# The order of the 24 products of a projected piece: low parts of the weights last

## The chip, the cores and the metric

The kernel runs on one core of a Trainium2 chip. The metric is device time in microseconds (us), from one launch. The engines are named as the profile names them: PE (TensorE, matrix products), PEld (its weight loads), DVE (VectorE), ACT (ScalarE), POOL (GpSimd) and SP (SyncE, which only issues DMAs here).

## What is computed

One layer of a hybrid sequence model on 1024 frames plus 16 learned ones (L = 1040), model width 1024. A normalised input goes through one combined projection, three groups of heads mix it in time, each in its own way, and one output projection brings it back.

```python
hn = rms_norm(h, norm_pre[l])
proj = jnp.einsum("bld,dp->blp", hn, w_in[l])
p_a, p_b, p_c = jnp.split(proj, _splits([P_A, P_B, P_C]), axis=-1)
mixed = jnp.concatenate([
    gated_deltanet_group(p_a, ...),   # 6 heads of 128
    rwkv7_group(p_b, ...),            # 8 heads of 64
    mamba2_group(p_c, ...),           # 12 heads of 64
], axis=-1)
out = jnp.einsum("blm,md->bld", mixed, w_out[l])
h = h + rms_norm(out, norm_post[l])
```

## The kernel before

**The projection.** The projected channels are cut into 61 tiles of 128. A tile is projected by `proj` in two or three pieces of 320 to 512 frames, each into a PSUM tile `pj` of its own (tag "proj", four of them). To keep float32 precision with fast products, the input is held as a rounded part `hh` and a low part `hl`, the weights as a rounded part `w[:, 0]` and a low part `w[:, 1]`, and a piece is the sum of three kinds of products over eight slices `kt` of 128 input channels: rounded weights with `hh`, rounded weights with `hl`, low parts with `hh`. That makes 24 products for a piece, accumulated in one PSUM tile.

**The weights.** `weights` (L143 to L155) fetches a tile in two halves (slices 0 to 3 and 4 to 7), `w_0` and `w_1`. For each half SP loads `raw`, ACT writes the negative of the rounded part to `w[:, 1]` (L151), then the rounded part to `w[:, 0]` (L152), and a DMA issued by POOL adds the float32 weights onto `w[:, 1]` (L153), which leaves the low part. There are four such buffers, so two tiles' weights; a half's buffer is free when the last product that reads it has run. The next tile's weights are asked for after the first piece of a tile (`self.prefetch`).

**What follows a piece.** `evac` empties the PSUM tile on ACT and DVE: a short convolution (`conv`, L179 to L187) or a token shift (`shifted`, L613 and L614).

**The order of the work.** Heads are handled by generators (`unit_a`, `unit_b`, `unit_c` for the three groups, `unit_o` for the output projection). `schedule` calls one step of a scan, or one product of a tile, at a time, by a clock of its own that adds up the size of the products; so small products of the scans (64 by 64 and 32 by 32, in plain float32: `bsi`, `bu`, `bm`, `am` and so on) stand between the large ones of the projection. The framework's scheduler then lays the instructions of each engine in an order for good, by priorities and its own estimate of when operands are there; on the chip every engine runs its instructions in that order, with waits where an operand or a buffer is not there yet. Products called through the class `Meter` all carry line L97.

Of the kernel before, what the change touches and what calls it, by code (L numbers as in the profile page):

```python
# [22 lines left out]
KT = 8  # L23
# [78 lines left out]
class Trunk:  # L102
# [54 lines left out]
    def proj(self, i, pieces, evac, halo=0):  # L157

        w = self.fetched.pop(i, None) or self.weights(i)
        for n, (a, b) in enumerate(pieces):  # L160
            a0 = max(a - halo, 0)
            p = self.pp.tile([128, 512], F32, tag="proj", name=f"pj{i}_{n}")
            for kt in range(KT):
                for m, (x, h) in enumerate(((0, self.hh), (0, self.hl), (1, self.hh))):
                    self.engines[2].matmul(p[:, : b - a0], w[kt // 4][:, x, kt % 4, :], h[:, kt, a0:b],
                                           start=(kt == 0 and m == 0), stop=(kt == KT - 1 and m == 2))
                    yield
            with self.tc.high_priority(EVA):
                evac(p, a, b, a - a0)
            if n == 0:  # L170
                self.prefetch(i)
# [1227 lines left out]
```

## Time and profile before

| | |
|---|---|
| median of 3 runs | 1450.17 us (1448.45 to 1453.15) |
| the profiled execution | 1442.35 us, its span 1440.4 us |
| PE busy | 1389.7 us, 96% of the span |
| weight loads (PEld) | 1188.8 us, beside PE |
| DVE, ACT, POOL busy | 935.4, 719.9, 172.4 us |
| mean granted TensorE clock | 0.985 |

The span counts from the first to the last instruction of the program; the 1.95 us that the time has on top lie around it. The projection lasts from about 23 to 1223 us, and the output projection fills most of what is left. Matmul records overlap (a product's record is about twice as long as the distance to the next one), so PE's speed is read from start to start, and PE's busy share hides waits shorter than a record.

### The profile page before, as it was taken

The numbers are of one execution on the slowest core, as the hardware profiler recorded it, in microseconds if no ns is written. First come the engines' busy times: TensorE is split into PE (matmuls) and PEld (weight loads), VectorE is DVE, ScalarE is ACT, GpSimd is POOL, SyncE is SP. The second block draws the span as 40 slices with busy tenths as digits, with TensorE's granted clock in tenths as the row PEclk, the third lists the DMA queues.
The fourth block names the chain that finished last, engine by engine and source line by source line (L and its number), as shares of the span: only waits on it lengthen the run. The fifth ranks groups of instructions, "written<-read, shape, count | busy, mean of one in ns | idle before, by whom it ended". The sixth has DMA issues, their size and how long they took to land.

```text
span 1440.4 us, 28351 instructions
## 1 busy us (share of the span) xinstructions
PE 1389.7 (96%) x10801; PEld 1188.8 (83%) x10801; DVE 935.4 (65%) x2610; ACT 719.9 (50%) x2020; POOL 172.4 (12%) x223
## 2 busy tenths in 40 slices
PE   4999999999999999999999999999999999899997
PEld 4999888778788789979778898889998987677786
DVE  6548586467667348879625788655589876632663
ACT  6365445446364464545636655444666355632520
POOL 2111010000010011111001110001231110201000
PEclk9999999999999999999979999999999999999999
DMA  7354243213234143234422242234553322743861
GB/s 233 78 131 87 56 102 71 57 40 88 44 66 112 30 133 89 57 82 89 100 60 60 54 108 62 59 88 89 133 124 77 71 38 56 233 133 101 254 198 44
DMA packets 120458, 136.43 MB, mean 95 GB/s; under 512 B 39867, under 2 KB 72379, under 8 KB 120323
## 3 DMA queue, kind: packets, MB, share of 16 engines
q1 hardware_dynamic: 102755, 102.64, 24.1%
q0 software_dynamic: 17568, 31.99, 13.4%
q8 instruction: 85, 1.39, 0.4%
q14 instruction: 50, 0.41, 0.1%
HBM read 116.99 MB, written 17.60 MB: 93 GB/s over the span
## 4 chain that ended last, share of the span: by engine, by line
PE 78%; issue 6%; ACT 6%; DMA 4%; DVE 4%; POOL 0%; SPq 0%; DVEq 0%; ACTq 0%; POOLq 0%
PE pj L97 45%; PE po L97 5%; PE bsi L97 4%; PE bu L97 3%; PE bgr L97 3%; PE am L97 2%; PE aops L97 1%; PE cdg L97 1%; ACT bbt L97 1%; DMA or<-in_w_out_dram 1%; PE ads L97 1%; PE av L97 1%; DMA omrw<-d_mix 1%; PE aks L97 1%; PE agk L97 1%
## 5 line engine op out<-in xcount | busy, mean ns | idle before, releaser
L97 PE MATMUL pj<-hh,w 128*128 128x350 f32 (+7 forms) x2736 | 757.6, 348 | 0.2 <-ACT hh L264 0.2
L97 PEld LDWEIGHTS pj<-hh,w 128*128 128x128 f32 x2736 | 483.4, 190 | 25.7 <-issue 4.4
L97 PE MATMUL pj<-hl,w 128*128 128x350 f32 (+7 forms) x1368 | 474.8, 347 | 0.0
L97 PEld LDWEIGHTS pj<-hl,w 128*128 128x128 f32 x1368 | 260.2, 190 | 11.8 <-issue 1.2
L153 POOL DMA_DIRECT2D w<-in_wt_dram x122 | 106.5, 873 | 878.6 <-ACT w L151 600.5
L151 ACT ACTIVATE w<-wr 128x512 fp32r<-128x512 f32 x122 | 76.8, 630 | 72.7 <-PE pj L97 70.7
L97 PE MATMUL po<-ow,omw 128*128 128x512 f32 x408 | 97.7, 400 | 4.0 <-ACT omw L1088 3.2
L97 PEld LDWEIGHTS po<-ow,omw 128*128 128x128 f32 x408 | 77.5, 191 | 24.2 <-ACT omw L1088 3.6
L97 PE MATMUL po<-ow,ome 128*128 128x512 f32 x360 | 90.5, 402 | 2.1 <-ACT ome L1088 1.6
L97 PEld LDWEIGHTS po<-ow,ome 128*128 128x128 f32 x360 | 66.6, 189 | 17.7 <-ACT ome L1088 2.2
L152 ACT CAST w<-wr 128x512 fp32r<-128x512 f32 x122 | 74.4, 609 | 0.1
L97 DVE TENSOR_SCALAR buv<-bu,b_ib 128x64 f32<-128x64 f32 x68 | 19.2, 282 | 71.6 <-PE bu L97 71.5
L97 PE MATMUL bsi<-buv,bgm 64*64 64x64 f32 x784 | 63.0, 230 | 0.7 <-DVE b_s L97 0.2
L97 DVE TENSOR_TENSOR s_tmp<-alb 33x30 f32<-33x30 f32 (+9 forms) x180 | 57.0, 317 | 3.2 <-DMA alb<-d_l 1.9
L97 DVE TENSOR_TENSOR alb<-alb,s_tmp 33x30 f32<-33x30 f32 (+9 forms) x180 | 57.0, 317 | 3.0 <-POOL alb L97 1.6
L97 PEld LDWEIGHTS bsi<-buv,bgm 64*64 64x64 f32 x784 | 43.5, 136 | 16.5 <-issue 4.6
L184 DVE SCALAR_TENSOR_TENSOR cbc<-pj,pack,cbc 128x346 f32<-128x346 f32 (+4 forms) x72 | 41.1, 571 | 20.5 <-ACT cbc L181 19.7
L852 ACT COPY by<-bsi 64x64 f32<-64x64 f32 x128 | 26.5, 207 | 48.9 <-PE bsi L97 47.6
L1089 DVE TENSOR_TENSOR ome<-omre,ome 128x512 fp32r<-128x512 f32 (+2 forms) x40 | 22.5, 600 | 36.2 <-ACT ome L1088 36.1
L97 PE MATMUL bgr<-bar,bbk 64*64 64x128 f32 x544 | 45.4, 277 | 0.0
L97 PE MATMUL bu<-buv,bbt 64*64 64x64 f32 x512 | 42.4, 234 | 0.0
L184 DVE SCALAR_TENSOR_TENSOR cx<-pj,pack,cx 128x346 f32<-128x346 f32 (+2 forms) x54 | 31.1, 576 | 16.9 <-ACT cx L181 15.9
(324 smaller groups left out, 2390.3 us busy)
## 6 DMA issues: line engine op xcount, KB each, us to landing
wr<-in_wt_dram SPq DMA_DIRECT2D x122, 256.0 KB, 3.4
w<-in_wt_dram POOLq DMA_DIRECT2D x122, 256.0 KB, 4.8
or<-in_w_out_dram SPq DMA_DIRECT2D x32, 256.0 KB, 3.8
omrw<-d_mix SPq DMA_DIRECT2D x32, 256.0 KB, 3.9
clt<-d_cs SPq DMA_DIRECT2D x24, 256.0 KB, 4.9
omre<-d_mix SPq DMA_DIRECT2D x24, 256.0 KB, 2.8
btw<-d_tw SPq DMA_DIRECT2D x8, 544.0 KB, 5.9
x<-in_x_dram SPq DMA_DIRECT2D x8, 512.0 KB, 7.7
```

The costliest lines, as they stand in the source:

```text
L97: return op(out, *args, **kw)
L151: nc.scalar.activation(w[:, 1], raw, AF.Copy, scale=-1.0)
L152: nc.scalar.copy(w[:, 0], raw)
L153: nc.gpsimd.dma_start(w[:, 1], src, accum_op=ADD)
L184: nc.vector.scalar_tensor_tensor(acc[:, a + z: b], p[:, o + z - s: o + b - a - s], cw[:, 3 - s: 4 - s], acc[:, a + z: b], MUL, ADD)
L852: nc.scalar.copy(yt[hs[(c - 1) % 2], (c - 1) // 2, hs[h]], pq[hs[h], 64:128])
L1089: nc.vector.tensor_tensor(t[:, 1], raw, t[:, 0].bitcast(F32), SUB)
```

## The change

The 24 products of a piece get another order. Before, each slice `kt` had its three kinds in turn. Now the 16 products with the rounded weights come first, over all eight slices, and then the eight with the low parts.

```diff
-            for kt in range(KT):
-                for m, (x, h) in enumerate(((0, self.hh), (0, self.hl), (1, self.hh))):
-                    self.engines[2].matmul(p[:, : b - a0], w[kt // 4][:, x, kt % 4, :], h[:, kt, a0:b],
-                                           start=(kt == 0 and m == 0), stop=(kt == KT - 1 and m == 2))
-                    yield
+
+            steps = [(kt, 0, h) for kt in range(KT) for h in (self.hh, self.hl)] + [(kt, 1, self.hh) for kt in range(KT)]
+            for j, (kt, x, h) in enumerate(steps):
+                self.engines[2].matmul(p[:, : b - a0], w[kt // 4][:, x, kt % 4, :], h[:, kt, a0:b],
+                                       start=(j == 0), stop=(j == len(steps) - 1))
+                yield
```

No instruction is added or removed on any engine. Line numbers behind this place are higher by one in the changed kernel.

**First place: PE, the second half of a piece that nothing interrupts** (`pj_1_636` is the piece, `w_0_581` and `w_1_587` its tile's two halves). Before:

```order
L97 MATMUL pj_1_636<-hl,w_0_581 128x350
L97 MATMUL pj_1_636<-hh,w_0_581 128x350
L97 MATMUL pj_1_636<-hh,w_1_587 128x350
L97 MATMUL pj_1_636<-hl,w_1_587 128x350
L97 MATMUL pj_1_636<-hh,w_1_587 128x350 x2
L97 MATMUL pj_1_636<-hl,w_1_587 128x350
L97 MATMUL pj_1_636<-hh,w_1_587 128x350 x2
```

With the change:

```order
L97 MATMUL pj_1_636<-hl,w_0_581 128x350
L97 MATMUL pj_1_636<-hh,w_1_587 128x350
L97 MATMUL pj_1_636<-hl,w_1_587 128x350
L97 MATMUL pj_1_636<-hh,w_1_587 128x350
L97 MATMUL pj_1_636<-hl,w_1_587 128x350
L97 MATMUL pj_1_636<-hh,w_1_587 128x350
L97 MATMUL pj_1_636<-hl,w_1_587 128x350
L97 MATMUL pj_1_636<-hh,w_1_587 128x350
L97 MATMUL pj_1_636<-hl,w_1_587 128x350
L97 MATMUL pj_1_636<-hh,w_0_581 128x350 x4
L97 MATMUL pj_1_636<-hh,w_1_587 128x350 x4
```

The last product that reads the first half `w_0` was the 12th of the 24 and is now the 20th; the last that reads `w_1` is still the 24th.

**Second place: ACT, from the 54th row of its order on, during the first DeltaNet tile** (`pj_0_593`, `pj_1_636` and `pj_2_667` are its pieces, `w_0_766` is the first half of a later tile, which takes over the buffer of `w_0_581`). Before:

```order
L151 ACTIVATE w_0_766<-wr_0_767 128x512
L353 ACTIVATE sc_ecs<-sc_cs 128x162
L152 CAST w_0_766<-wr_0_767 128x512
L179 ACTIVATE ak_580<-pj_0_593,pack 128x348
L179 ACTIVATE ak_580<-pj_1_636,pack 128x346
```

With the change:

```order
L354 ACTIVATE sc_ecs<-sc_cs 128x162
L180 ACTIVATE ak_580<-pj_0_593,pack 128x348
L180 ACTIVATE ak_580<-pj_1_636,pack 128x346
L352 ACTIVATE sc_kd<-sc 128x54
L353 ACTIVATE sc_kdt<-sc 128x108
L355 ACTIVATE sc_etot<-pcl 128x162
L151 ACTIVATE w_0_766<-wr_0_767 128x512
L180 ACTIVATE ak_580<-pj_2_667,pack 128x346
L152 CAST w_0_766<-wr_0_767 128x512
```

The write to `w_0_766` stood ahead of the emptying of the first two pieces and now stands behind it.

**Third place: ACT and PE in the middle of the program, at an RWKV tile** (`bv` is the tile's result, `pj_1_7922` its second piece, `bvT` are transposes of `bv` on PE, `buv` is where ACT copies them, `cyT` are transposes of another head). ACT before:

```order
L97 COPY buv_0_8133<-bvT_0_8135 64x64 x2
L613 ACTIVATE bv_7362<-pj_1_7922,mu_321 128x384
L97 COPY buv_0_8133<-bvT_1_8151 64x4x64 x3
L97 ACTIVATE cz_6619<-cyT_00_7691,pack 128x512
L97 ACTIVATE cz_6620<-cyT_01_7720,pack 128x512
```

ACT with the change:

```order
L614 ACTIVATE bv_7362<-pj_1_7922,mu_321 128x384
L97 COPY buv_0_8133<-bvT_0_8135 64x64 x2
L97 COPY buv_0_8133<-bvT_1_8151 64x4x64 x4
L97 ACTIVATE cz_6619<-cyT_00_7691,pack 128x512
L97 ACTIVATE cz_6620<-cyT_01_7720,pack 128x512
```

The emptying of the second piece stood behind the copies to `buv` and now stands ahead of them. PE before, in the third piece:

```order
L97 MATMUL cyT_00_7691<-pack,cx_0_5817 128x128
L97 MATMUL cyT_01_7720<-pack,cx_0_5817 128x128
L97 MATMUL pj_2_8048<-hh,w_0_7706 128x322
L97 MATMUL pj_2_8048<-hl,w_0_7706 128x322
L97 MATMUL pj_2_8048<-hh,w_0_7706 128x322 x2
L97 MATMUL bvT_1_8151<-pack,bv_7362 128x128
```

PE with the change:

```order
L97 MATMUL pj_2_8048<-hh,w_1_7712 128x322
L97 MATMUL pj_2_8048<-hl,w_1_7712 128x322
L97 MATMUL bvT_1_8151<-pack,bv_7362 128x128 x2
L97 MATMUL bvT_9_8172<-pack,bv_7362 128x128
L97 MATMUL pj_2_8048<-hh,w_1_7712 128x322
L97 MATMUL pj_2_8048<-hl,w_1_7712 128x322
```

Ten products of the third piece stand ahead of `bvT_1` in both; the two `cyT` have moved behind it, and `bvT_9` has come forward, ahead of the piece's last 14 products.

## Rows read from the trace of the kernel before

**Rows 1.** The page: busy engines, and the chain that ended last.

```profile
PE 1389.7 (96%) x10801; PEld 1188.8 (83%) x10801; DVE 935.4 (65%) x2610; ACT 719.9 (50%) x2020; POOL 172.4 (12%) x223
...
PE 78%; issue 6%; ACT 6%; DMA 4%; DVE 4%; POOL 0%; SPq 0%; DVEq 0%; ACTq 0%; POOLq 0%
```

**Rows 2.** Engines by stretch, 60 to 1225 us: the sum's row.

```profile
sum 1165.00, PE 1150.80 PEld 995.11 DVE 792.80 ACT 610.00 POOL 144.18; mean PE 191.80 PEld 165.85 DVE 132.13 ACT 101.67 POOL 24.03
```

**Rows 3.** PE's waits: who it waited for, us in total, times, longest.

```profile
PE bvT L97 <- DVE bv L614: 2.6, 1, 2.6
...
PE bbT L97 <- ACT bbt L97: 1.5, 5, 0.4
...
PE bu L97 <- ACT b_x L97: 1.0, 2, 0.7
...
PE pj L97 <- ACT hh L264: 0.2, 1, 0.2
```

**Rows 4.** Timeline of PE at 601 us: start, length, instruction, count.

```profile
600.86 0.32 PE L97 MATMUL pj<-hl,w 128*128 128x350 f32 x1
...
601.34 0.32 PE L97 MATMUL pj<-hl,w 128*128 128x350 f32 x1
601.50 0.38 PE L97 MATMUL akT<-pack,ak 128*128 128x128 f32 x2
601.64 0.56 PE L97 MATMUL pj<-hh,w 128*128 128x350 f32 x2
602.04 0.32 PE L97 MATMUL pj<-hl,w 128*128 128x350 f32 x1
```

**Rows 5.** Timeline of PE: second to fifth product of the first piece.

```profile
25.25 0.63 PE L97 MATMUL pj<-hl,w 128*128 128x336 f32 x1
25.67 0.48 PE L97 MATMUL pj<-hh,w 128*128 128x336 f32 x1
...
26.66 0.63 PE L97 MATMUL pj<-hh,w 128*128 128x336 f32 x1
27.09 0.47 PE L97 MATMUL pj<-hl,w 128*128 128x336 f32 x1
```

**Rows 6.** ACT's waits for PE at the weights, and ACT's timeline at 65 us.

```profile
ACT w L151 <- PE pj L97: 70.7, 36, 9.6
...
65.48 0.63 ACT L151 ACTIVATE w<-wr 128x512 fp32r<-128x512 f32 x1 [9.55 <-PE pj L97]
66.02 0.32 ACT L353 ACTIVATE sc_ecs<-sc_cs 128x162 f32<-128x162 f32 x1
```

**Rows 7.** Timelines of SP, ACT, DVE and PE at 685 to 694 us.

```profile
684.73 0.28 SPq L758 DMA_DIRECT2D d_t<-blb  x1
691.85 1.33 SPq L760 DMA_DIRECT2D bgm<-d_t  x3
...
691.90 0.42 ACT L97 COPY buv<-bvT 64x64 f32<-64x64 f32 x2 [5.73 <-issue]
692.35 0.58 ACT L613 ACTIVATE bv<-pj,mu 128x384 f32<-128x384 f32 x1
...
692.96 0.62 DVE L614 SCALAR_TENSOR_TENSOR bv<-pj,pack,bv 128x384 f32<-128x384 f32 x1 [2.87 <-ACT bv L613]
...
688.85 0.31 PE L97 MATMUL pj<-hl,w 128*128 128x322 f32 x1
...
690.61 0.46 PE L97 MATMUL pj<-hh,w 128*128 128x322 f32 x2
693.63 0.47 PE L97 MATMUL bvT<-pack,bv 128*128 128x128 f32 x1 [2.56 <-DVE bv L614]
```

**Rows 8.** Engines by stretch around two falls of the clock (PEclk: share granted).

```profile
693.00:696.40 3.40, 2.77 (x12) 2.68 (x13) 1.95 (x7) 1.58 (x4) 0.00 (x0) 0.50 0.45 69
...
720.30:723.70 3.40, 3.40 (x81) 2.81 (x79) 0.26 (x1) 1.47 (x5) 0.00 (x0) 1.00 0.39 159
723.70:740.80 17.10, 17.10 (x103) 12.30 (x104) 1.93 (x7) 4.89 (x15) 0.86 (x1) 0.50 0.17 32
```

## Prediction

> **What bounds the kernel now.** I read the page first. PE is busy for 1389.7 us of 1440.4, and the chain of work that ended last is 78% PE; ACT stands at half the span and POOL at an eighth [rows 1]. Records of products overlap, so I looked next at how much time PE has nothing in flight: in the whole projection stage, 60 to 1225 us, it is 1165.0 − 1150.8 = 14.2 us, or 1.2% of the stage [rows 2]. The list of PE's waits tells what ended the longer ones. No row of it names a DMA or the weights: the only one at `pj` is 0.2 us, for `hh` [rows 3]. So PE runs an order that was fixed when the program was built, almost without a gap, and its time is the sum of its products, of what it costs to pass between kinds of products, and of the granted clock. A change that adds and removes nothing can move the time in three ways: by a wait it takes away or adds, by more or fewer passages between kinds, and by what the clock makes of the new mixture.
>
> **The products themselves.** In the timeline at 601 us three products of 350 columns, rounded with `hh`, low with `hh` and rounded with `hl` among them, take 601.34 − 600.86 = 0.48 us from start to start, 0.16 us each whatever the kind [rows 4]. Each has its own weight load: 10801 loads for 10801 products [rows 1]. The order of the kinds inside an undisturbed piece is therefore worth nothing, either way; 24 products stay 24 times 0.16 us.
>
> **The low parts are needed later.** They come last of a half's operands, by way of two ACT instructions and POOL's DMA. Before, the third product of a piece reads them, now the 17th, 14 products or 14 × 0.16 = 2.2 us later. That is worth something only where PE waited for them. The place where it is likeliest is the first piece, whose weights have just been fetched: its second product starts at 25.25 and its third, the first that reads low parts, at 25.67, 0.42 us on. But two products further, where nothing new is read, the same distance is 27.09 − 26.66 = 0.43 us [rows 5]. So nothing was waited for even there, and in the remaining tiles, prefetched a tile ahead, the list of waits shows none. I cost this at 0. What covers it before is the prefetch; if that cover were thin, the gain could be at most the 0.2 us of rows 3 and what hides inside a record.
>
> **The first half's buffer comes free later.** Its last reader moves from the 12th to the 20th product of the tile's last piece, 8 × 0.16 = 1.3 us later. Who waits for it is ACT at L151, which waited for PE 36 times, 70.7 us in all, before; at 65.48 us it had waited 9.55 us, with `sc_ecs` and the emptying of two finished pieces behind it in its order [rows 6]. In the new order those stand ahead (the second place of the change), so the wait at L151 begins later and holds back less. PE feels neither yet: its waits for ACT in rows 3 are 1.5, 1.0 and 0.2 us, and four PSUM tiles let it go on for some pieces without an emptying. Then the load is 1.3 us later, and the low part, whose need has moved by 2.2 us, has more room than before. I cost this at 0, with bounds of −1.0 (the 1.0 us at `bu` goes) and +4.0 (what ACT's lateness costs PE, 1.5 + 1.0 + 0.2 = 2.7, comes once and a half again).
>
> **Interruptions of the projection.** Counted in the built orders, the stream of `pj` products is broken by other products 566 times before and 571 times now. What one costs is in rows 4: from the product at 601.34 to that at 602.04 are 0.70 us, in which three `pj` products (0.48 us) and two of 128 columns run. Charged nothing for the work of the two, the interruption costs 0.22; charged 128/350 of 0.16 us each, 0.12 in all, it costs 0.10. Five more come to +0.5 to +1.1 us; I take +0.8. Passages between other kinds of products become fewer by some (1617 changes of the tile's name before, 1600 now); at 0 to 0.1 us each that is −1.7 to 0, and I take 0, because most of them are between small products that follow each other densely.
>
> **The stall at 691 us**, the longest of the stage, is where the order itself changes a wait. Before, ACT stood 5.73 us at the first copy to `buv`, until a DMA (`d_t<-blb`, issued at 684.73) had landed: SP's next DMA, which reads what it wrote, went out at 691.85, and the copy began at 691.90. Behind the copy stood the emptying of `pj_1`, whose piece had ended by 688.85 [rows 7]. So `bv` came from ACT at 692.93 and from DVE at 693.58, and `bvT_1` ran at 693.63, after 2.56 us in which PE had nothing. In the new order ACT empties `pj_1` ahead of the copies, at about 689.0, and `bvT_1` can run by 690.8. What is late next is `bvT_9`, the second row behind it on PE, which needs the PSUM tile that the first two copies empty: 691.90 + 0.42 = 692.32. By then PE has done the same ten products and two transposes as it had before at 693.63, so the gain is 693.63 − 692.35 = 1.3 us. It is 0 if the DMA lands as much later, 2.7 (2.56 and the 0.17 that is left open ahead of it, as an estimate from the same rows) if nothing stands in the way. I take −1.3.
>
> **The clock.** [...] My sum takes 0 for the clock: the small products stand as close together in the new order at both places, and a shorter stall remains.
>
> **The sum.** 0 + 0 + 0.8 + 0 − 1.3 + 0 = −0.5 us. From the profiled execution, 1442.35 us (its span of 1440.4 and 1.95 around it), that makes 1441.85. That execution was 7.8 us below the median of the runs, 1450.17, so the same step from the median gives 1449.7 us. With the bounds of the parts (−1.0 to +4.0, +0.5 to +1.1, −1.7 to 0, −2.7 to 0) taken to half their width together, the likeliest case's own range is 1446.5 to 1453.5.
>
> **Rivals.**
> *Faster.* The new order closes most of PE's gaps, because ACT no longer stands at L151 ahead of work that is ready. Everything that PE has open in the stage is 14.2 us [rows 2]; half of it gone and the falls of the clock behind the stalls with it (1.7 us) makes −7 − 1.7, about 1441.5. For it speaks the second place of the change, which is one of 36 such waits; against it that hardly any of PE's waits in rows 3 is for a piece's emptying.
> *Slower by the clock.* The place is the stretch of small products of a DeltaNet head beside an RWKV head's, where PE before spent 17.1 us at half clock. A second stretch of that kind, or one twice as long, costs what the half clock takes from 17.1 us, half of them: +8.5, 1458.7. It decides from 8.8 more microseconds at half clock (+4.4). For it speaks that such stretches come with every DeltaNet head; against it that the order there has hardly changed.
> *Slower by the buffers.* L151 waits 1.3 us longer for each of the 61 first halves, at worst 79 us more of waiting on ACT, on top of 70.7. It decides once ACT's copies in the RWKV steps are late, where PE waits for ACT now for 1.0 us. If all of PE's 2.7 us of waits for ACT grow in the ratio (70.7 + 79) / 70.7, and reach some of the other gaps, it is +2 to +6: about 1455. Against it speaks that the scheduler put L151 further back in ACT's order.
>
> **How the numbers follow.** A measurement of this kernel tells a difference from none at about 0.3%, 4.4 us here: the three runs spread over 4.7. My forecast has 0.50, the faster rival 0.25, the clock 0.14, the buffers 0.11. Some of the buffers' case stays within 0.3%, so: faster 0.26, same 0.52, slower 0.22. The range reaches to the faster rival's near side and to the clock's: 1442 to 1458.5 us.
>
> **What would show it.** In the changed kernel's profile three `pj` products in a row should still take 0.48 us at 350 columns, with no row that names the weights among PE's waits. The wait at `bvT` near 691 us should be about 1.3 us, at `bvT_9`, and the stage 60 to 1225 us should have 12 to 16 us of open time on PE. ACT's waits at L151 for PE should lie between 40 and 110 us. The forecast is wrong if the time at half clock in the projection stage changes by more than 9 us, or if a new wait of over 3 us appears on PE's list.

## The result, and the profile after

The changed kernel takes 1457.23 us (median; 1447.79 to 1463.90), the kernel before, beside it on the same chip, 1446.74 (1441.99 to 1462.96). The ratio is 1.0067, with a 95% interval of 1.0051 to 1.0083: slower by some 9.7 us. Two later comparisons gave 1.0054 (1.0030 to 1.0078) and 1.0059 (1.0027 to 1.0090). The forecast was no change.

The profiled execution took 1460.2 us, 17.9 more than the one of before. First its page:

```profile
PE 1402.6 (96%) x10801; PEld 1202.5 (82%) x10801; DVE 935.8 (64%) x2610; ACT 720.5 (49%) x2020; POOL 170.6 (12%) x223
...
PEclk9999998999999999999969999999999999999999
...
PE 76%; issue 7%; ACT 6%; DVE 6%; DMA 4%; POOL 1%; SPq 0%; DVEq 0%; ACTq 0%; POOLq 0%
```

The same 10801 products keep PE busy for 12.9 us longer than in [rows 1]. PE's and ACT's waits (who waits, for whom, us in total, times, longest):

```profile
PE czT L97 <- DVE ctmp L97: 3.4, 1, 3.4
...
PE bvT L97 <- ACT buv L97: 2.6, 1, 2.6
PE cbT L97 <- ACT cbt L97: 2.2, 1, 2.2
...
PE bm L97 <- DVE bdd L791: 1.7, 1, 1.7
...
ACT w L151 <- PE pj L97: 63.0, 33, 6.7
```

In the profile of before, `czT` has no row, and the other two were shorter:

```profile
PE bm L97 <- DVE bdd L790: 0.9, 1, 0.9
...
PE cbT L97 <- ACT cbt L97: 0.3, 1, 0.3
```

In a second profile of before `cbT` waited 1.1 us. `bvT` waits as long as in [rows 3], but for ACT's copy, and no row names the weights. The timelines of PE, DVE and ACT around the first two:

```profile
679.75 0.32 PE L97 MATMUL pj<-hh,w 128*128 128x346 f32 x1
679.91 0.32 PE L97 MATMUL pj<-hl,w 128*128 128x346 f32 x1
680.07 0.32 PE L97 MATMUL pj<-hh,w 128*128 128x346 f32 x1
680.23 0.32 PE L97 MATMUL pj<-hl,w 128*128 128x346 f32 x1
683.92 0.52 PE L97 MATMUL czT<-pack,cz 128*128 128x128 f32 x3 [3.38 <-DVE ctmp L97]
...
702.48 0.44 PE L97 MATMUL bvT<-pack,bv 128*128 128x128 f32 x2
705.50 0.48 PE L97 MATMUL bvT<-pack,bv 128*128 128x128 f32 x1 [2.58 <-ACT buv L97]
...
681.67 0.56 DVE L185 SCALAR_TENSOR_TENSOR av<-pj,pack,av 128x346 f32<-128x346 f32 x1
682.16 0.37 DVE L97 TENSOR_TENSOR s_tmp<-blb 68x220 f32<-68x220 f32 x1
682.46 0.56 DVE L185 SCALAR_TENSOR_TENSOR av<-pj,pack,av 128x346 f32<-128x346 f32 x1
682.95 0.36 DVE L97 TENSOR_TENSOR blb<-blb,s_tmp 68x220 f32<-68x220 f32 x1
683.24 0.54 DVE L97 SCALAR_TENSOR_TENSOR ctmp<-ctmp,czT 128x384 f32<-128x384 f32 x1
...
701.17 0.58 ACT L614 ACTIVATE bv<-pj,mu 128x384 f32<-128x384 f32 x1 [1.40 <-PE pj L97]
705.02 1.19 ACT L97 COPY buv<-bvT 64x64 f32<-64x64 f32 x4 [3.27 <-DMA d_t<-blb]
```

Three products of 346 columns still take 680.23 − 679.75 = 0.48 us, as in [rows 4]. At 680 us DVE works without a pause, on a convolution (`av`) and on `solve32` (`s_tmp`, `blb`), and `ctmp` stands behind both in its order; PE waits 3.38 us. At 703 us the emptying of `pj_1` now runs before the copies to `buv`, as the order had it, but the copies wait for the same DMA as in [rows 7], so `bvT_9` waits 2.58 us where `bvT_1` had waited 2.56. Engines by stretch, PEclk the share of the clock granted:

```profile
701.40:704.80 3.40, 1.52 (x11) 1.15 (x9) 3.13 (x16) 0.35 (x1) 0.00 (x0) 1.00 0.27 92
704.80:708.20 3.40, 2.70 (x11) 2.64 (x12) 0.66 (x3) 1.88 (x6) 0.00 (x0) 0.50 0.32 50
728.70:732.10 3.40, 3.40 (x64) 2.56 (x60) 0.78 (x3) 1.68 (x4) 0.00 (x0) 1.00 0.50 198
732.10:759.40 27.30, 27.30 (x204) 20.68 (x205) 3.40 (x12) 8.24 (x25) 0.86 (x1) 0.50 0.07 22
...
sum 1165.00, PE 1147.80 PEld 997.27 DVE 784.72 ACT 599.19 POOL 139.67; mean PE 1147.80 PEld 997.27 DVE 784.72 ACT 599.19 POOL 139.67
```

The long stretch at half clock (PEclk 0.50) lasts 27.3 us, 17.1 in [rows 8], and again follows a stretch in which PE was never idle. Two more profiles of the changed kernel have 27.3 and 20.5 us there, a second one of before 20.5, so single profiles overlap. The last line is 60 to 1225 us: 17.2 us without a product in flight, 14.2 in [rows 2]. But the projection now ends at 1241 us and not at 1222, so the same products are compared over these two stretches, before and changed:

```profile
23.00:1223.00 1200.00, 1185.62 (x9908) 1026.94 (x9906) 812.59 (x2279) 625.81 (x1814) 147.40 (x196) 0.99 0.35 79
```

```profile
23.00:1241.00 1218.00, 1198.60 (x9907) 1040.41 (x9905) 812.50 (x2279) 626.17 (x1813) 145.13 (x195) 0.97 0.34 78
```

That is 14.4 us without a product in flight before and 19.4 now. The stretches at half clock within them add up to 34.1 us before and 64.7 now; the second profiles of both kernels have 47.7 us each, the third of the changed kernel 64.7.

**Two shares.** Every execution comes with its span and its mean granted clock. *Lost* below is span × (1 − clock), what the half clock takes if PE's speed sets the end; *rest* is the span less that. The span indeed follows it: among 159 executions of the kernel before (mean clocks from 0.966 to 0.987) it grows by 0.71 us for each us lost, among 44 of the changed one by 0.80. So *lost* overstates by about a quarter, and *rest* is low by as much where *lost* is high. Three executions that were slow, over 1.5% above the fastest of their kernel, are left out: two of `w_0` free late (with them lost is 28.1, rest 1415.5) and one of before with wide products (28.6 and 1425.3). Means with their standard errors, us:

| kernel | executions | span | lost | rest |
|---|---|---|---|---|
| before | 159 | 1446.6 ± 0.3 | 27.0 ± 0.4 | 1419.6 ± 0.2 |
| changed | 44 | 1454.8 ± 0.8 | 31.8 ± 0.9 | 1423.0 ± 0.3 |
| low parts last in each half | 12 | 1447.0 ± 1.1 | 28.1 ± 1.2 | 1418.9 ± 0.5 |
| old kinds, changed kernel's order | 24 | 1450.2 ± 0.6 | 28.6 ± 0.7 | 1421.6 ± 0.3 |
| new kinds, PE in before's order | 8 | 1455.6 ± 1.1 | 26.9 ± 1.4 | 1428.7 ± 0.5 |
| new kinds; PE, DVE, SP in before's order | 12 | 1455.1 ± 1.3 | 27.3 ± 1.4 | 1427.8 ± 0.3 |
| old kinds, `w_0` free late | 22 | 1442.2 ± 1.3 | 26.6 ± 1.5 | 1415.6 ± 0.3 |
| the same, four waits moved | 24 | 1442.7 ± 1.3 | 29.1 ± 1.4 | 1413.6 ± 0.4 |
| changed, low parts in own buffers | 6 | 1467.7 ± 1.4 | 40.9 ± 1.7 | 1426.9 ± 0.5 |
| changed, four waits moved | 12 | 1448.4 ± 0.9 | 26.9 ± 0.8 | 1421.5 ± 0.3 |
| before, four waits moved | 12 | 1441.9 ± 1.4 | 22.0 ± 1.2 | 1419.9 ± 0.5 |
| before, four waits made longer | 12 | 1452.4 ± 0.7 | 28.2 ± 1.1 | 1424.2 ± 0.7 |
| before, 22 wide products added | 11 | 1452.7 ± 1.1 | 27.1 ± 1.4 | 1425.6 ± 0.6 |
| changed, 22 wide products added | 6 | 1465.5 ± 1.9 | 37.9 ± 2.4 | 1427.7 ± 0.9 |

The changed kernel loses 8.2 us: 3.4 of rest and 4.8 of clock. At 0.80 us for each us lost, the clock makes 3.8 of them and 4.4 are left for the rest.

The executions come from several chips. The rest of the kernel before is the same on each (1419.0 to 1420.0 us), but its loss is 26.0 to 26.5 in five of six sets and 29.9 ± 1.4 in one, so differences of the loss of 3 us or less should be read with care. On each of the two chips with both, the changed kernel lost more than before beside it: 30.9 against 26.4 and 32.8 against 26.0.

### The profile page after: what moved, and what is told of

It is laid out like the page before. It is cut to its first block, busy times and chain, and to the rows that moved or that the text cites. A ratio compares the mean times of both kernels' runs of the same rounds, so it can differ in the third digit from the quotient of the medians.

```text
span 1458.2 us, 28337 instructions
## 1 busy us (share of the span) xinstructions
PE 1402.6 (96%) x10801; PEld 1202.5 (82%) x10801; DVE 935.8 (64%) x2610; ACT 720.5 (49%) x2020; POOL 170.6 (12%) x223
## 4 chain that ended last, share of the span: by engine, by line
PE 76%; issue 7%; ACT 6%; DVE 6%; DMA 4%; POOL 1%; SPq 0%; DVEq 0%; ACTq 0%; POOLq 0%
PE pj L97 41%; PE po L97 7%; PE bsi L97 4%; PE bu L97 3%; PE bgr L97 3%; PE am L97 2%; ACT bbt L97 2%; PE cdg L97 1%; PE aops L97 1%; PE ads L97 1%; DMA x<-in_x_dram 1%; PE av L97 1%; PE agk L97 1%; PE agq L97 1%; PE aks L97 1%
## 5 line engine op out<-in xcount | busy, mean ns | idle before, releaser
L97 PEld LDWEIGHTS pj<-hh,w 128*128 128x128 f32 x2736 | 487.7, 192 | 26.4 <-issue 3.9
L97 PEld LDWEIGHTS pj<-hl,w 128*128 128x128 f32 x1368 | 264.8, 194 | 12.1 <-issue 1.7
L151 ACT ACTIVATE w<-wr 128x512 fp32r<-128x512 f32 x122 | 76.7, 628 | 69.3 <-PE pj L97 63.0
L152 ACT CAST w<-wr 128x512 fp32r<-128x512 f32 x122 | 74.4, 610 | 0.1
L853 ACT COPY by<-bsi 64x64 f32<-64x64 f32 x128 | 26.4, 206 | 63.6 <-PE bsi L97 62.2
L97 DVE TENSOR_TENSOR s_tmp<-blb 68x30 f32<-68x30 f32 (+14 forms) x120 | 38.5, 321 | 8.4 <-DMA blb<-d_l 7.3
```

The source lines that it names most:

```text
L97: return op(out, *args, **kw)
L151: nc.scalar.activation(w[:, 1], raw, AF.Copy, scale=-1.0)
L152: nc.scalar.copy(w[:, 0], raw)
L853: nc.scalar.copy(yt[hs[(c - 1) % 2], (c - 1) // 2, hs[h]], pq[hs[h], 64:128])
```

## The experiments

The theories are those of the expectations. A: the new order of the instructions makes the loss, by the clock. B: the kinds make it. C: a fixed part of about 3 us, and chance for the rest. D: kinds and order together bring the clock down. E: the late release makes it. F: the waits of the particular order make it. G: such waits cost little by themselves, but each is a pause that can bring the clock down.

**Kinds or order?** The change does three things: another order of the kinds, a later release of `w_0` (from the 12th to the 20th product), and an order of all engines that the scheduler makes anew. Where an order is *held*, a chain of ordering links of the class `NoSync` between an engine's successive instructions gives it the order of another build:

```diff
+    for seq in zlib.decompress(base64.b85decode(ORDER)).decode().split("\n"):
+        n, last = 0, None
+        for d in seq.split():
+            n += int(d)
+            i = made[f"I-{n}"]
+            if last is not None:
+                tc.add_manual_dep(i, last, mybir.DependencyInfo(mybir.DependencyClass.NoSync, mybir.DependencyReason.DATA), reason="order")
+            last = i.name
...
         Trunk(tc, args).run()
+        _pin(tc)
```

*The kernel before once more*, no edit.

> The kernel before once more, as a measure of how much two readings of one program differ and of how its time goes with its granted clock. Both theories: 1447 us, ratio to the kernel before 1.000 within 0.002. Theory A (the new order of the instructions costs the clock, the kinds themselves cost nothing) also expects that in its executions the time rises as the mean granted clock falls, by about 7 us for 0.01 of clock.

Measured: 0.9987 (0.9966 to 1.0008). Its twelve executions had mean clocks from 0.976 to 0.986 and took 1442.9 to 1454.6 us, the longer ones at the lower clocks.

*Low parts last in each half.*

```diff
-            steps = [(kt, 0, h) for kt in range(KT) for h in (self.hh, self.hl)] + [(kt, 1, self.hh) for kt in range(KT)]
+            steps = []
+            for g in (range(4), range(4, 8)):
+                steps += [(kt, 0, h) for kt in g for h in (self.hh, self.hl)] + [(kt, 1, self.hh) for kt in g]
```

> Each half of a piece (four slices, one weight buffer) takes its eight products with rounded weights first and its four with the low parts last, so that w_0 comes free at the twelfth product as before the change. The order of the instructions on all five engines comes out as in the kernel before but for the kinds inside the pieces. Theory A: as before, 1447 us within 4, ratio 1.000 within 0.003. Theory B (the kinds' own order or the wait for the low parts costs the time): about half of the loss or more stays, 1452 us or above, ratio 1.003 or more.

Measured: 0.9986 (0.9960 to 1.0012). With the release and the order of all engines as before, low parts last cost nothing.

*The old kinds, with all five orders of the changed kernel held*, twice, the second time beside the changed kernel:

> The three kinds in turn as before the change, with each engine's instructions held in the order that they have in the changed kernel. Theory A: the loss is there without the new kinds, 1457 us within 4, ratio 1.007 within 0.003, mean granted clock about 0.975. Theory B: the loss is gone, 1447 us within 4, ratio 1.000 within 0.003, clock 0.985.

> Once more the three kinds in turn with all five orders of the changed kernel, beside the changed kernel itself on one chip. If the order alone makes the loss (theory A, which the first reading of 1.0004 spoke against): the same ratio as the changed kernel within 0.002, about 1.005. If kinds and order each make a part: 1.001 to 1.003, 3 us or more below the changed kernel.

> The changed kernel once more, on the chip of the next three. Theory A as first put (the new order alone costs the clock) fell with the old kinds in the new order, which lost 0.0004. What is left: theory C, that the changed kernel has about 3 us more of waits that no clock explains (span less the time lost to the half clock: 1423 against 1419) and that the rest of its loss is how often the clock happened to fall in its executions; then the ratio is 1.002 to 1.004 and the mean granted clock within 0.001 of that of the kernel before. Theory D, that kinds and order together bring the clock down: ratio 1.006 to 1.008 and a mean clock lower by 0.003 or more.

> The changed kernel a third time, for the comparison with the run ahead of it: ratio 1.0055 within 0.0025 to the kernel before, mean granted clock lower by 0.003.

Measured: 1.0004 (0.9980 to 1.0028) and 1.0033 (1.0009 to 1.0056) for the order with the old kinds; 1.0054 and 1.0059 for the changed kernel. The two readings of the order have nearly the same span (1449.7 and 1450.6 us); it is before, beside the first, that stood at its high loss of 29.9. A in its first form fell. B fits the first reading, but not the second, nor the run ahead, where kinds changed without the release cost nothing. In the changed kernel's second reading the mean clock, 0.979 against 0.982, was as D had it, and in the third as well, 0.978 against 0.982; the ratio 1.0054 lies between C's range and D's. In the table the order alone makes 2.0 us of rest and 1.6 of loss; the kinds on top of it 1.4 of rest and 3.2 ± 1.1 of loss. On the one chip that had both, the loss was 32.8 ± 2.4 and 29.3 ± 1.1, so the share of the kinds in the loss is likely, not certain. The order's own waits are there with the old kinds:

```profile
PE czT L97 <- DVE ctmp L97: 3.4, 1, 3.4
...
PE bvT L97 <- ACT buv L97: 2.4, 1, 2.4
PE cbT L97 <- ACT cbt L97: 1.7, 1, 1.7
```

*The new kinds, with orders of before held*: on PE alone, then on PE, DVE and SP. With ACT held too, its wait for `w_0` would stand ahead of emptyings that PE needs first, so by the two orders the program could not end; no run shows it.

> The changed kernel (rounded weights first over the whole piece, low parts last) with TensorE's instructions held in the order of the kernel before; the other engines keep an order of their own. Theory A in its narrow form, that TensorE's order alone sets the clock: 1447 us within 5, ratio 1.000 within 0.004. Theory B: 1457 us, ratio 1.007. A time over 1457 would say that holding TensorE to an order that the other engines don't keep costs waits of its own, to be seen among TensorE's waits.

> The changed kernel's kinds over the whole piece, with TensorE, VectorE and SyncE held in the order of the kernel before; ScalarE and GpSimd keep an order of their own, in which the writes of the weights stand later. Theories A and C (the kinds and the later weights cost nothing, the order does): ratio 1.000 within 0.003. Theory B (the kinds' order or the lateness of the weights costs): ratio 1.004 or more.

Measured: 1.0054 (1.0027 to 1.0081) and 1.0065 (1.0041 to 1.0090). The clock is that of before (lost 26.9 ± 1.4 and 27.3 ± 1.4 us, 27.0 ± 0.4 in before); the rest is longer by 9.1 and 8.2 us. PE's order is that of before, so the starts of its products can be compared one by one (each less half of the half-clock time ahead of it): the second kernel falls behind in steps of 0.4 to 1.2 us, several of them at products that wait for ACT or DVE. Some of PE's waits, from its list (in the profile of before they were 0.9, 1.6, 0.2 and 0.7 us):

```profile
PE bm L97 <- DVE bdd L791: 2.4, 2, 2.1
PE aoT L97 <- DVE avt L97: 2.4, 3, 1.8
...
PE agq L97 <- ACT aqT L97: 2.0, 4, 0.9
PE akT L97 <- ACT akT L97: 1.7, 4, 0.9
```

So in orders made for the earlier release the new kinds with the later one cost 8 to 9 us of rest, and the scheduler's new order avoids about half of that. How much of it the release makes, and how much that held engines and free ones follow orders made apart, is not separated. The expectation had named the second for a time over 1457, and the first of the two took 1458.24. One such wait, for DVE, is in its list; it is gone where DVE is held too:

```profile
PE csr L363 <- DVE csrow L365: 3.1, 1, 3.1
```

**Is it the release, then?** *The old kinds with the slices in another order*, so that `w_0` comes free at the 21st product; twice:

```diff
-            for kt in range(KT):
+            for kt in (0, 1, 2, 4, 5, 6, 3, 7):
```

> The three kinds in turn as before the change, but the eight slices in the order 0, 1, 2, 4, 5, 6, 3, 7, so that w_0 comes free at the 21st product instead of the twelfth and nothing else of the change is there; the scheduler orders the engines anew. Theory E, that the later release of w_0 makes the loss (by other waits, and by an order in which the clock falls more): ratio 1.003 to 1.009, span less the time lost to the half clock 1422 us or more against 1419. Theory B, that the order of the kinds makes it: 1.000 within 0.002.

> The kernel with w_0 free late and the three kinds in turn once more, for the comparison with the run ahead of it and because its time without the clock (1415.5 against 1419.9) was below that of the kernel before: ratio 0.997 to 1.000, time without the clock 1415 to 1417.

Measured: 0.9985 (0.9954 to 1.0016) and 0.9969 (0.9946 to 0.9992), with 4.0 us less of rest than before. ACT waits at the weights as in the changed kernel, and nothing is lost. PE does wait for a tile's weights there, which it did not in before, but for 0.4 us only:

```profile
ACT w L151 <- PE pj L97: 63.7, 37, 9.5
...
PE pj L97 <- DMA w<-in_wt_dram: 0.4, 1, 0.4
```

Theory E fell: a late release alone need not cost anything. It leads to another order, and that order may be a better one.

*The changed kernel with rounded and low parts in buffers of their own:*

```diff
-            w = self.wp.tile([128, 2, 4, 128], F32R, tag="w", name=f"w{i}_{h}", bufs=NW)
+            w = [self.wp.tile([128, 4, 128], F32R, tag="w" + t, name=f"w{t}{i}_{h}", bufs=n) for t, n in (("h", 3), ("l", 5))]
...
-                self.engines[2].matmul(p[:, : b - a0], w[kt // 4][:, x, kt % 4, :], h[:, kt, a0:b],
+                self.engines[2].matmul(p[:, : b - a0], w[kt // 4][x][:, kt % 4, :], h[:, kt, a0:b],
```

> The changed kernel with the rounded weights and the low parts of a half in buffers of their own, three and five of them, in the same memory: the rounded part of w_0 is free at the eighth product, the low part at the twentieth, but it has one buffer more. The scheduler orders the engines anew. Theory E (the late release makes the loss): the loss goes, ratio 1.000 within 0.003. Theory B (the kinds make it): 1.005. A ratio below 0.997 would make it the fastest of these kernels, which no theory asks for.

Measured: 1.0145 (1.0111 to 1.0180). It brings a wait of its own, at L152, for the three buffers of the rounded parts, and with it again another order; so it fits neither theory's number and doesn't tell them apart.

```profile
ACT wh L152 <- PE pj L97: 74.4, 65, 8.6
```

**The waits.** *The changed kernel, before, and the one with `w_0` free late, each with four waits moved*: the five orders are held, and the next products of the projection are brought ahead of the instruction that waits. One of the places, in PE's order:

```diff
 L97 MATMUL pj_1_7718<-hl,w_1_7520 128x346
-L97 MATMUL czT_3_7541<-pack,cz_6619 128x128
-L97 MATMUL czT_3_7541<-pack,cz_6620 128x128
-L97 MATMUL czT_3_7541<-pack,cz_6922 128x128
 L97 MATMUL pj_1_7718<-hh,w_1_7520 128x346
...
 L97 MATMUL pj_2_7796<-hl,w_0_7514 128x344
+L97 MATMUL czT_3_7541<-pack,cz_6619 128x128
+L97 MATMUL czT_3_7541<-pack,cz_6620 128x128
+L97 MATMUL czT_3_7541<-pack,cz_6922 128x128
```

> The changed kernel with its five orders held but for four places on TensorE: the next 10, 18, 14 and 11 products of the projections are brought ahead of the instructions that wait at 459 (bm, 1.7 us), 681 (czT, 3.4), 703 (bvT, 2.6) and 1051 us (cbT, 2.2). Theory E (the late release) fell with the kernel that frees w_0 late and lost nothing. Theory F: the changed kernel's loss is what its particular order of instructions brings, and its waits at a few places are most of the part that no clock explains: up to 9.9 us come back, span less the time lost to the half clock 1414 to 1418 us against 1423, ratio to the kernel before 0.998 to 1.002. Rival: the engines waited for are late either way and the waits turn up behind the products that were brought forward: 1.004 to 1.006.

> The same done to the kernel before at its own places: 5, 6, 14 and 6 products brought ahead of bm at 456 (0.9 us), cof at 546 (0.9), bvT at 691 (2.6) and cbT at 1040 us (0 to 1.1). By theory F 4 to 5 us come back, and the fall of the clock that follows the wait at 691 may go with it (another 1.7): ratio 0.995 to 0.998. Rival: 1.000.

> The kernel with w_0 free late and the three kinds in turn, its orders held, with 6, 9, 11 and 13 products brought ahead of cds at 536 (1.0 us), cof at 550 (1.5), bvT at 695 (1.9) and cbT at 1030 us (2.3). By theory F up to 6.7 us come back: span less the time lost to the half clock 1409 to 1412 us against 1415.5, ratio 0.993 to 0.996, and the fastest of these kernels. Rival: as without the moves, 0.998.

> The kernel with the three kinds in turn, w_0 free late and four waits moved once more, since it had the lowest time: ratio 0.995 to 0.998, span less the time lost to the half clock 1413 to 1415 us.

Measured: 1.0025 (1.0007 to 1.0043) for the changed kernel, 0.9970 (0.9943 to 0.9997) for before, 0.9970 (0.9942 to 0.9998) and 0.9991 (0.9964 to 1.0018) for the third. In the changed kernel 6.4 of the 8.2 us come back, but otherwise than theory F had it (a rest of 1414 to 1418): 4.9 of them are clock and only 1.5 rest. Of the 9.9 us of waits more than half are still there, in part at the instructions behind:

```profile
PE czT L97 <- DVE ctmp L97: 2.1, 2, 1.7
...
PE bbon L97 <- ACT buv L97: 1.3, 2, 1.0
...
PE bm L97 <- DVE bdd L791: 0.7, 1, 0.7
PE cbT L97 <- ACT cbt L97: 0.6, 1, 0.6
PE avT L97 <- DVE ctmp L97: 0.6, 1, 0.6
```

Before gains 5.0 us of clock (4.2 beside before on the same chip) and nothing of rest, so its ratio lies in F's range without F's reason. The third is another case: 2.0 us of rest come back, of the up to 6.7 that F asked for, and the loss does not fall, 29.1 ± 1.4 against 26.6 ± 1.5; both its ratios lie above F's range. From 650 to 760 us, where two of the four places lie, the granted clock was 0.84 in the changed kernel and 0.89 with the waits moved. That doesn't show the gain by itself, for the third profile of the changed kernel has 0.89 there too; in this order, the changed kernel, the moved one and the changed kernel's third:

```profile
650.00:760.00 110.00, 103.73 (x762) 87.45 (x760) 64.29 (x217) 53.30 (x157) 10.11 (x14) 0.84 0.32 74
```

```profile
650.00:760.00 110.00, 105.42 (x856) 88.14 (x855) 66.98 (x225) 56.61 (x175) 10.50 (x15) 0.89 0.33 78
```

```profile
650.00:760.00 110.00, 103.78 (x806) 87.55 (x805) 66.03 (x221) 56.24 (x165) 10.51 (x15) 0.89 0.34 78
```

*Before, with four waits made longer*: the same edit the other way, 10, 4, 10 and 8 products of the projection put behind the waiting instruction.

> The opposite of the run that moved the waits of the kernel before: its five orders held, but bm at 456, cof at 546, bvT at 691 and cbT at 1040 us are put 10, 4, 10 and 8 products of the projections earlier, so that TensorE waits there about 6 us longer in all (32 products of 0.19 us). Theory G: such waits cost little by themselves, since what is waited for is late either way, but each pause can bring the clock down; then span less the time lost to the half clock stays at 1419 to 1421 us and the time lost rises from 27 to 30 to 33 us, ratio 1.002 to 1.005. Rival 1: the waits cost their own length: 1424 to 1426 us, with the time lost unchanged. Rival 2: neither, 1.000.

Measured: 1.0042 (1.0023 to 1.0060); rest +4.6 us, lost +1.2 ± 1.2. That is rival 1, and theory G fell in this direction: longer pauses cost their own length and bring no measurable further loss of the clock. The waits did not grow by the 6 us that were meant: `bvT`, `bm` and `cof` below had 2.6, 0.9 and 0.9 us in before, and `cbT`, 0.3 and 1.1 in two profiles of it, has 1.4, in all some 4 us.

```profile
PE bvT L97 <- DVE bv L614: 3.4, 1, 3.4
...
PE bm L97 <- DVE bdd L790: 2.5, 1, 2.5
PE cof L97 <- DVE clt L97: 1.7, 1, 1.7
```

**Small products and the clock.** *22 wide products among the small ones of `bm` and `am`, whose results nobody reads, the five orders held*, in before and in the changed kernel. The help function and one of six places:

```diff
+    def wide(self, out):
+        self.nc.tensor.matmul(out, self.hh[:, 0, 0:128], self.hh[:, 1, 0: out.shape[1]], start=True, stop=True, skip_group_check=True)
...
+                if p == 3 and c % 3 == 2:
+                    self.wide(p1[:, 288:512])
```

> The kernel before, its five orders held, with 22 products of 224 to 512 columns added among the narrow products of bm and am between 707 and 731 us; their results are read by nobody, so the output is the same. They cost 6336 columns, 2.9 us at the full clock by 0.16 us for 350. If narrow products standing together bring the clock down, the fall of 17 to 20 us at 724 goes, which gives back up to 8.5 to 10 us: about 1442 us, ratio 0.996 within 0.003. If the clock falls for another reason, the cost alone stays: 1450 us, ratio 1.002.

> The same 22 products in the changed kernel, its five orders held; output unchanged. If narrow products standing together bring the clock down, the fall of 27 us at 732 goes, worth up to 13.7 us less 2.9: 1446 to 1450 us, ratio to the kernel before 0.998 to 1.001. Otherwise 1458 to 1460 us, ratio 1.007 to 1.009.

Measured: 1.0044 (1.0022 to 1.0066) and 1.0121 (1.0088 to 1.0155), both above what either side expected; in the changed kernel the loss by the clock even rose, 37.9 ± 2.4 against 31.8. The long fall stayed; before with wide products, around its start and in it:

```profile
727.40:730.80 3.40, 3.40 (x43) 2.38 (x42) 0.28 (x1) 1.05 (x2) 0.00 (x0) 1.00 0.54 216
730.80:754.70 23.90, 23.90 (x167) 16.90 (x166) 1.49 (x5) 5.64 (x16) 0.86 (x1) 0.50 0.12 23
```

That small products close together bring the clock down is not shown by this, nor excluded: the wide ones were few, and they delayed the stretch that they stood in.

## Why the prediction was wrong

It said "My sum takes 0 for the clock: the small products stand as close together in the new order at both places, and a shorter stall remains." The places are the two falls of [rows 8], at 693 and 723 us; that the closeness of small products sets the clock was the author's assumption, which no run shows. The step failed: 4.8 us of the 8.2 are there, about 3.8 at 0.80 us for each. The other 4.4 stand against −0.5 for all the remaining terms; there the gain at the stall did not come, and the waits of the new order were missing, as told below.

It is the rival *Slower by the clock*, given 0.14, that comes nearest, but its 1458.7 beside the measured 1457.23 is in good part luck. It took +8.5 of clock alone, from a base of 1450.2 that 20 executions put at 1446.7. Its place was right in part: the stretch that it named is longer in the first pair of profiles by 27.3 − 17.1 = 10.2 us, where the time at half clock in the whole projection grew by 64.7 − 34.1 = 30.6, and the other profiles have 27.3 and 20.5 in the changed kernel and 20.5 in before.

The faster rival's 1.7 us, for falls of the clock that go with the stalls, is shown by no run; it is half of the 3.40 us at 0.50 behind the stall in [rows 8], an estimate. In the changed kernel the stall stayed (2.58 us), and so did 3.40 us at 0.50 behind it; where four waits were made longer, the loss was 28.2 ± 1.1 us against 27.0 ± 0.4.

Two of the signs of being wrong came: a new wait of over 3 us, and more than 9 us of change at half clock. The second could not decide from a pair of profiles, since two of before differ by 47.7 − 34.1 = 13.6 us. The sum's base hid this as well: a mean clock from 0.966 to 0.987 of one program moves its time by over 20 us, and 0 was taken for a term of which no row gave the size. The open time on PE, 17.2 us, is also outside the 12 to 16 that the text asked for.

*The products themselves*, 0: right (0.48 us for three).

*The low parts are needed later*, 0: right. No row of PE's waits names the weights, and with the low parts last in each half the ratio is 0.9986.

*The first half's buffer comes free later*, 0 with a bound of +4.0: right in that a late release alone need lose nothing (4.0 us less of rest in the kernel with `w_0` free late), and ACT's wait at L151 stayed between 40 and 110 us. But it was covered by a new order only. In orders of before it costs, kinds and mismatched orders included, 8 us, twice the bound; PE waits there oftener and longer for ACT and DVE. The bound was low by its reading as well: it took 2.7 us of PE's waits for ACT, from three rows, and the list of before has seven shorter rows for ACT ahead of the output projection, 2.4 us together. The price of the remedy, another order of every engine, has no term in the sum.

*Interruptions*, +0.8, and *fewer passages*, 0: together with all else in the order, the old kinds in the new order have 2.0 ± 0.4 us more of rest. Its waits at `czT` and `cbT`, 3.4 and 1.7 us, are larger than that, so something else may have become shorter, by up to 3 us. That was not separated further.

*The stall at 691*, −1.3: the place was right and the gain was not there. PE waits at `bvT_9` for ACT's copies, as the text had it; but the DMA they need landed later too, 705.02 − 701.17 = 3.85 us after the emptying of `pj_1` began, where the text had 691.90 − 689.0 = 2.9: most of the way to the case that the text put at 0. Beside it the order brought the wait of over 3 us that the text named as a sign of being wrong, at `czT`, where DVE has two other streams ahead.

*The range of the likeliest case*, 1446.5 to 1453.5, does not follow from its parts: their bounds add up to −4.9 and +5.1, and half of that width is 5.0 us, not 7.0.

Open is what makes the clock fall more in the changed kernel. That pauses of PE do it is shown in part only: with pauses moved away the loss went from 31.8 to 26.9 us and from 27.0 to 22.0, but in the kernel with `w_0` free late from 26.6 to 29.1; and with longer pauses it was 28.2 ± 1.1 against 27.0. In before and in the changed kernel the longest falls come with no pause ahead of them (3.40 of 3.40 us busy). With `w_0` free late the longest stands at another place, and PE was busy for 2.53 of the 3.40 us ahead:

```profile
461.80:465.20 3.40, 2.53 (x74) 1.83 (x74) 1.32 (x3) 0.66 (x2) 0.00 (x0) 0.99 0.52 172
465.20:485.70 20.50, 20.50 (x157) 14.88 (x158) 4.46 (x12) 5.64 (x18) 0.00 (x0) 0.50 0.00 1
```

A share of 3.2 ± 1.1 us seems to follow the kinds, in one and the same order. No single feature of the orders tried explains losses from 22.0 to 40.9 us.

## What to carry to other kernels

Where a scheduler fixes the order when the program is built, an edit that adds and removes nothing is first of all a new order: build it, and hold the old order in the new code and the new order in the old code before saying what the edit costs. Ten orders of this work (one of them with other buffers) differ by 15 us of rest and 19 us of lost time, so a forecast from the edit alone should be wide, and an order that is better by luck (here `w_0` free late, 4.0 us less of rest than before) says nothing about its edit. Read clock and rest apart, over many executions; a pair of profiles can differ by more than the effect.

## What the runs showed of the hardware

A product of 224 to 512 columns among small ones cost more than its columns: 22 of them made the rest longer by 1425.6 − 1419.6 = 6.0 us in before, 0.27 us each, and by 4.7 ± 0.9 us in the changed kernel, where 0.16 us for 350 columns had given 2.9 in all. The timeline shows it, in before with wide products: the next small product starts 723.25 − 722.95 = 0.30 us after a wide one of 224 columns.

```profile
722.95 0.37 PE L124 MATMUL bm<-hh 128*128 128x224 f32 x1
723.25 0.31 PE L97 MATMUL bm<-bgm,bdd 32*32 32x32 f32 x6
```

Moving the projection's products ahead of a wait gave back clock rather than waiting time in two of three kernels: 5.0 us of it in the kernel before, where the rest stayed at 1419.9, and 4.9 in the changed one, with 1.5 of rest. In the kernel with `w_0` free late it gave back 2.0 us of rest and no clock.
